# A hybrid decoder layer on one core: 32 groups by seven products instead of 25, with part of their sums on POOL

## The chip, the cores and the metric

The kernel runs on one core of a Trainium2 chip. The engines of the core that matter here are PE (TensorE: matmuls, and its weight loads, PEld), DVE (VectorE: elementwise work), ACT (ScalarE: elementwise work and copies), POOL (GpSimd: elementwise work) and SP (SyncE, which here only issues DMAs). SBUF is the memory on the core that all of them read and write; PSUM is the memory into which PE accumulates. The metric is the device time of one execution in microseconds; smaller is better.

## The reference

One decoder layer over 256 tokens and 2048 features, in float32. After an RMS norm one projection gives the inputs of a state-space mixer and of an attention mixer. Their outputs, 2048 features each, stand beside each other, and a matrix of 4096 x 2048 projects them out. A second RMS norm, a residual, and then an MLP:

```
mix = hybrid_mixer(rmsnorm(h, norm_mix_pre[i]), ...)      # ends in einsum('bse,ed->bsd', y_mix, w_out)
h = h + rmsnorm(mix, norm_mix_post[i])
hdn = relu(einsum('bsd,df->bsf', u, w_up))
ff = einsum('bsf,fd->bsd', hdn * hdn, w_down)             # w_down: 8192 x 2048
h = h + rmsnorm(ff, norm_mlp_post[i])
```

The change touches only the multiplications by w_out and w_down: activations of 256 tokens times weights, summed over 4096 and 8192 features.

## The kernel before, in words

**Two parts for each number.** A float32 matmul is done on operands split in two: `hi` is the value rounded to PE's faster format (ACT, line 136), `lo` is the rest (DVE, line 137, a subtraction of two operands in SBUF). A product is three matmuls: hi by hi, hi by lo, lo by hi. A matmul takes a 128x128 block of activations and a 128x512 block of weights.

**A plain group.** The sum over features goes in groups of 256 (two blocks of 128, KB = 2), and the output columns in blocks of 512. `row_tiles` does one group for one column block: a 512 KB tile of weights (`raw`) is loaded, split into a `hi` and a `lo` tile, and multiplied with both token blocks: 2 token blocks x 2 feature blocks x 3 matmuls = 12. `unit` treats two column blocks at once, so a plain group there has 24 matmuls and two raw tiles.

**A group by seven products.** For two token blocks, two feature blocks and two column blocks a group is a 2x2 by 2x2 block multiplication, eight products. `seven` (line 278) does it by Winograd's scheme with seven, 21 matmuls. For that it needs sums of blocks. Of the weights: with the raw tiles a and b, `e[:,0]` = a0 + b0, `e[:,1]` = e0 + b1, `t4` = e1 + a1, and b0 + b1 in place: four 128x512 additions on DVE (line 194), then splits of a, e, b (128x1024 each) and t4 (128x512), four hi/lo pairs. Of the activations: `sums_of_acts` (line 257 on) joins hi and lo (L269), takes three sums (L270 to L272) and splits the four results (L136, L137). These sums are kept in `room["sums"]` and used again when the second pair of column blocks comes. The seven products go partly into extra accumulators (`more`); a combination behind the last seven of a unit (`combine_new`, `combine_onto`) adds them up.

**The units.** There are six calls of `unit` with such groups: w_out, first and second pair of column blocks (lines 877 and 888); w_down's first 4096 rows (957, 959); its last 4096 rows (979, 983). Each has its order of groups with the list of those done by seven, and some last plain groups. Before these come five plain groups of w_out, beside which the attention ends.

**What sets the order.** The first part of every loop is the scheduler's: it places each instruction by priority and by its own estimate. The work on weights has a raised priority (AHEAD). For the groups in question `in_line` also puts each split and each addition of weights behind the last one on ACT and on DVE (`line`), so their order is that of the program. Loads go through SP's queue in program order. There are five pairs of hi and lo (BUFS), so a pair can be written only when PE is done with the pair five before. Of raw tiles there are four (RAWS), and, while the tile `u` of the layer's input isn't needed (w_out and the last part of w_down), three more in its memory. The memory of `u` holds the sums too: ten blocks (SUMS), two for each group. In the first part of w_down the memory of `h` holds eight (SUMS_H), and there are four raw tiles. The scratch tile `e` has one buffer, `r` (`tmp`) two; `wpost`, two tiles of 128x512, holds a norm's weights.

Of the kernel before, what the change touches and what calls it, by code (L numbers as in the profile page):

```python
# [10 lines left out]
F32 = mybir.dt.float32  # L11
F32R = mybir.dt.float32r
# [4 lines left out]
P = 128  # L17
# [31 lines left out]
WARM = 6  # L49
STAY = 4  # L50
SUMS = 10
SUMS_H = 8
FINE = 4


# [19 lines left out]
def hymba_layer(ctx: ExitStack, tc: tile.TileContext, x, norm_mix_pre, w_in, conv_w, conv_b, dt_bias, a_log,  # L75
# [17 lines left out]
    us = []  # L93

    def new_u():
        us[:] = [big.tile([P, n, 2, S], F32R, name=name) for n, name in ((SUMS, "ua"), (NK - SUMS, "ub"))]

    def u(k):

        return us[k // SUMS][:, k % SUMS]  # L100

    new_u()
    sh = big.tile([P, NK, S], F32R, name="sh")
# [43 lines left out]
        return raw  # L147


    room = {}  # L150

    def in_place_of_u():
        room["sums"] = big.tile([P, SUMS, 2, S], F32R, name="ua")
        room["raw"] = big.tile([P, NK - SUMS, NB], F32, name="ub")
        room["turn"] = 0
        sums_of.clear()

    def in_place_of_h():
        room["sums"] = hp.tile([P, SUMS_H, 2, S], F32R, name="h")
        room["raw"] = None  # L160
        sums_of.clear()

    def fetch_next(src, k0, c0):

        if room["raw"] is None:
            return fetch(src, k0, c0)
        n = KB * (room["turn"] - RAWS)
        room["turn"] = (room["turn"] + 1) % (RAWS + (NK - SUMS) // KB)
        return fetch(src, k0, c0, into=None if n < 0 else room["raw"][:, n:n + KB])

    def parts():
# [87 lines left out]
    def sums_of_acts(k):  # L259

        if k in sums_of:
            return sums_of[k]
        q = KB * len(sums_of)
        assert q < room["sums"].shape[1]
        h_, l_, r = part(k * KB)
        with tc.high_priority(offset=AHEAD):
            a, c = (tmp().rearrange("p (i s) -> p i s", s=P) for _ in range(2))
            ah_, al_ = (v[:, r:r + KB].bitcast(F32).rearrange("p j (t s) -> p (j t) s", t=NT) for v in (h_, l_))
            nc.vector.tensor_tensor(a, ah_, al_, op=ALU.add)  # L269
            nc.vector.tensor_tensor(c[:, 0:2], a[:, 0::3], a[:, 1:2].to_broadcast([P, 2, P]), op=ALU.subtract)  # L270
            nc.vector.tensor_tensor(c[:, 2], a[:, 0], c[:, 1], op=ALU.add)
            nc.vector.tensor_tensor(c[:, 3], a[:, 2], c[:, 2], op=ALU.subtract)  # L272
            ch, cl = (room["sums"][:, q + j].rearrange("p b (t s) -> p (b t) s", t=NT) for j in range(KB))
            split(ch, cl, c)
        sums_of[k] = ch, cl
        return ch, cl

    def seven(src, ca, cb, k, acc, more, first, last):
# [4 lines left out]
        with tc.high_priority(offset=AHEAD):  # L283
            raw_a = fetch_next(src, k * KB, ca)
            raw_b = fetch_next(src, k * KB, cb)
            e, t4 = hp.tile([P, KB, NB], F32, name="e"), tmp()
            add_in_line(e[:, 0], raw_a[:, 0], raw_b[:, 0])
            add_in_line(e[:, 1], e[:, 0], raw_b[:, 1])
            hl_a = parts()
            split_in_line(*hl_a, raw_a)  # L290
            add_in_line(t4, e[:, 1], raw_a[:, 1])
            add_in_line(raw_b[:, 0], raw_b[:, 0], raw_b[:, 1])
            hl_e = parts()
            split_in_line(*hl_e, e)
            hl_b = parts()
            split_in_line(*hl_b, raw_b)
            hl_t = parts()
            split_in_line(*(v[:, 0] for v in hl_t), t4)
# [66 lines left out]
                nc.vector.tensor_tensor(dst[:, f], a[:, 0], dst[:, f], op=ALU.add)  # L365

    def act_u(k):
        t = us[k // SUMS]
        return t[:, :, 0], t[:, :, 1], k % SUMS


    sq1 = cp.tile([P, NT, 4], F32, name="sq1")
# [501 lines left out]
    def order_of(ks, by_seven):  # L874
        return [(k, k in by_seven) for k in ks]

    unit(w_out, 0, order_of(range(early, 14), (6, 9, 12)), (14, 15), acc, more,
         lambda x: combine_new(0, x), 0, (whole(0), whole(1)), first=False)
    for n in (2, 3):
        load_wpost(norm_mix_post, n)  # L880
# [2 lines left out]
    def third(t, a):  # L883
# [1 line left out]
        first3.append(sums_but_last(ssq, t))  # L885

    first3 = []
    unit(w_out, 2, order_of((0, 1, 6, 2, 9, 3, 12, 5, 4, 7, 8, 10), (6, 9, 12, 4, 8)), (11, 13, 14, 15), acc, more,
         lambda x: combine_new(2, x), LAG_OUT, (third, done), 2)


# [47 lines left out]
    for hf in range(2):  # L939
# [14 lines left out]
        if hf == 0:  # L954
            in_place_of_h()
            acc, more = [bank() for _ in range(2 * NT)], [psmall(), bank(), psmall(), bank()]
            unit(w_down, 0, order_of(range(14), (4, 7, 10, 13)), (14, 15), acc, more,
                 lambda x: combine_new(0, x), 0, (onto(0), onto(1)))
            unit(w_down, 2, order_of((0, 1, 4, 2, 3, 7, 5, 6, 10, 8, 9, 13), (4, 7, 10, 13)), (11, 12, 14, 15), more, acc,
                 lambda x: combine_new(2, x), 0, (onto(2), onto(3)))  # L960
            h = hp.tile([P, NT, D], F32, name="h")

# [45 lines left out]
```

## Time and profile before

| what | before |
|---|---|
| median of 3 runs (lowest to highest) | 1496.34 us (1496.32 to 1499.82) |
| the profiled execution | 1494.86 us |
| its span, first to last instruction | 1493.1 us |
| mean granted clock of TensorE | 0.996 |
| matmuls | 7650 |
| busy: PE, DVE, ACT, POOL | 99%, 72%, 54%, 4% |
| the six units: w_out, w_down's first part, its last part | from 642 to 782, 968 to 1136, 1315 to 1483 us |

A row of the timeline has the start in us from the span's beginning, the duration in us, the engine, the line of the kernel, the operation, output<-inputs by their names in the program, and the shape; in brackets stands the idle time in front of it and what ended it. Matmuls overlap in the pipeline, so their spacing is the difference between starts. A row of a group has after the bar the busy time in us and the mean duration in ns, and then the idle time before.

### The profile page before, as it was taken

How to read it: one execution, taken by the hardware profiler on the slowest of the kernel's cores; microseconds unless marked ns; L12 is line 12 of the kernel's file. 1: busy time of each engine (PE TensorE's matmuls, PEld its weight loads, DVE VectorE, ACT ScalarE, POOL GpSimd, SP SyncE). 2: the span in 40 equal slices, each digit the busy share in tenths (PEclk: the TensorE clock that was granted, in tenths of full speed). 3: DMA queues.
4: the chain of work that ended last, by engine and by line, in shares of the span. 5: the costliest groups of instructions: out<-in, count | busy, mean ns of one | idle time of the engine just before them, and what ended most of it. 6: DMA issues, size and time to landing. Idle time of an engine off the chain costs nothing.

```text
span 1493.1 us, 20429 instructions
## 1 busy us (share of the span) xinstructions
PE 1477.8 (99%) x7650; PEld 1262.5 (85%) x7650; DVE 1075.3 (72%) x1582; ACT 806.0 (54%) x1125; POOL 56.9 (4%) x73
## 2 busy tenths in 40 slices
PE   9999999999999999999999999999999999999997
PEld 8888888888888888888878888888888888888886
DVE  6988897886555555587978656578775665678896
ACT  7574565455545454555556555545554554555552
POOL 0002200220000000000000000000000000000101
PEclk9999999999999999999999999999999999999999
DMA  7665666555656565575556666545568666656562
GB/s 275 196 201 181 182 185 189 179 169 169 178 167 178 170 171 180 204 247 199 199 188 208 194 189 190 185 169 197 200 213 273 189 184 194 187 203 206 198 214 97
DMA packets 151012, 287.35 MB, mean 192 GB/s; under 512 B 11664, under 2 KB 14592, under 8 KB 150656
## 3 DMA queue, kind: packets, MB, share of 16 engines
q1 hardware_dynamic: 143312, 272.37, 57.9%
q10 hardware_dynamic: 7600, 13.68, 2.7%
q8 instruction: 60, 0.98, 0.3%
q14 instruction: 40, 0.33, 0.1%
HBM read 281.78 MB, written 4.23 MB: 192 GB/s over the span
## 4 chain that ended last, share of the span: by engine, by line
PE 94%; DVE 2%; DMA 1%; ACT 1%; issue 1%; SPq 0%; POOL 0%; POOLq 0%; DVEq 0%; ACTq 0%
PE acc L341 29%; PE acc L344 15%; PE acc L242 11%; PE acc L243 11%; PE acc L241 10%; PE ps L242 2%; PE ps L241 2%; PE ps L243 2%; PE acc L312 2%; PE acc L311 2%; PE acc L313 2%; DVE lo L137 1%; PE ps L662 1%; PE ps L312 1%; PE ps L313 1%; PE ps L311 1%
## 5 line engine op out<-in xcount | busy, mean ns | idle before, releaser
L137 DVE TENSOR_TENSOR lo<-raw,hi 128x1024 fp32r<-128x1024 f32 (+1 forms) x466 | 569.5, 1225 | 313.2 <-ACT hi L136 306.7
L136 ACT ACTIVATE hi<-raw 128x1024 fp32r<-128x1024 f32 (+1 forms) x466 | 490.1, 1055 | 463.5 <-PE acc L341 239.6
L341 PE MATMUL acc<-ua,hi 128*128 128x512 f32 x1240 | 333.7, 399 | 0.8 <-DVE ua L139 0.8
L341 PEld LDWEIGHTS acc<-ua,hi 128*128 128x128 f32 x1240 | 217.6, 189 | 34.7 <-DVE ua L139 1.0
L341 PE MATMUL acc<-ub,hi 128*128 128x512 f32 x744 | 205.5, 397 | 0.0
L344 PEld LDWEIGHTS acc<-ua,lo 128*128 128x128 f32 x1240 | 182.0, 189 | 21.1
L344 PE MATMUL acc<-ua,lo 128*128 128x256 f32 x1240 | 187.2, 281 | 0.0
L341 PEld LDWEIGHTS acc<-ub,hi 128*128 128x128 f32 x744 | 127.2, 189 | 16.3 <-issue 0.2
L344 PEld LDWEIGHTS acc<-ub,lo 128*128 128x128 f32 x744 | 114.3, 189 | 15.8
L344 PE MATMUL acc<-ub,lo 128*128 128x256 f32 x744 | 118.1, 281 | 0.0
L241 PE MATMUL acc<-hi,sh 128*128 128x512 f32 x224 | 88.3, 394 | 0.0
L242 PE MATMUL acc<-lo,sh 128*128 128x512 f32 x224 | 87.3, 390 | 0.1
L243 PE MATMUL acc<-hi,sl 128*128 128x512 f32 x224 | 87.3, 390 | 0.0
L242 PE MATMUL acc<-lo,ah 128*128 128x512 f32 x208 | 81.0, 390 | 0.0
L243 PE MATMUL acc<-hi,al 128*128 128x512 f32 x208 | 80.9, 389 | 0.0
L241 PE MATMUL acc<-hi,ah 128*128 128x512 f32 x208 | 80.9, 389 | 0.0
L241 PE MATMUL acc<-hi,ua 128*128 128x512 f32 x180 | 71.2, 396 | 0.0
L242 PE MATMUL acc<-lo,ua 128*128 128x512 f32 x180 | 70.6, 392 | 0.0
L243 PE MATMUL acc<-hi,ua 128*128 128x512 f32 x180 | 70.5, 393 | 0.0
L137 DVE TENSOR_TENSOR lo<-ub,hi 128x1024 fp32r<-128x1024 f32 x48 | 58.4, 1221 | 16.5 <-ACT hi L136 15.8
L136 ACT ACTIVATE hi<-ub 128x1024 fp32r<-128x1024 f32 x48 | 50.2, 1056 | 36.5 <-PE acc L243 17.1
L136 ACT ACTIVATE hi<-e 128x1024 fp32r<-128x1024 f32 x25 | 26.6, 1062 | 47.0 <-DVE e L194 41.2
(315 smaller groups left out, 2114.4 us busy)
## 6 DMA issues: line engine op xcount, KB each, us to landing
raw<-in_w_in_dram SPq DMA_DIRECT2D x190, 512.0 KB, 3.6
raw<-in_w_up_dram SPq DMA_DIRECT2D x128, 512.0 KB, 3.7
raw<-in_w_down_dram SPq DMA_DIRECT2D x104, 512.0 KB, 4.4
raw<-in_w_out_dram SPq DMA_DIRECT2D x40, 512.0 KB, 4.1
ub<-in_w_out_dram SPq DMA_DIRECT2D x24, 512.0 KB, 4.2
ub<-in_w_down_dram SPq DMA_DIRECT2D x24, 512.0 KB, 4.5
bc<-acs_d ACTq DMA_DIRECT2D x8, 512.0 KB, 4.6
xs<-in_x_dram SPq DMA_DIRECT2D x8, 256.0 KB, 6.4
```

The lines of the kernel that those rows point to most:

```text
L136: return (nc.scalar.activation(hi, src, AF.Copy), nc.vector.tensor_tensor(lo, src, hi.bitcast(F32), op=ALU.subtract))
L137: nc.vector.tensor_tensor(lo, src, hi.bitcast(F32), op=ALU.subtract))
L241: nc.tensor.matmul(acc[t], a_h[:, r, ts], hi[:, j], start=begin, stop=False)
L242: nc.tensor.matmul(acc[t], a_h[:, r, ts], lo[:, j], start=False, stop=False)
L243: nc.tensor.matmul(acc[t], a_l[:, r, ts], hi[:, j], start=False, stop=end)
L311: nc.tensor.matmul(dst, a_h, hi[:, j], start=own and first, stop=False)
L312: nc.tensor.matmul(dst, a_h, lo[:, j], start=False, stop=False)
L313: nc.tensor.matmul(dst, a_l, hi[:, j], start=False, stop=own and last)
L341: nc.tensor.matmul(acc[f], hi[:, j, f * P:(f + 1) * P], u(k0 + j), start=k0 + j == 0, stop=False, skip_group_check=True)
L344: nc.tensor.matmul(acc[f][:, 0], lo[:, j, f * P:(f + 1) * P], u(k0 + j)[:, 0], start=False, stop=k0 + j == NK - 1, skip_group_check=True)
L662: nc.tensor.matmul(p[:, c, r], bc[:, r, c * P:(c + 1) * P], xdt[:, c, r], start=True, stop=True)
```

## The change

It does four things.

- 32 groups by seven in place of 25: the six units have 4, 6, 5, 5, 6, 6 where they had 3, 5, 4, 4, 4, 5. Between two sevens there is now mostly one plain group, where there were two in most units.
- In `seven`, two of the four additions of weights (b0 + b1, and t4) are given to POOL, and stand in front of a's split in the program; they are no longer in the line of DVE's instructions.
- In `sums_of_acts` the three sums behind the first go to POOL; joining hi and lo, and the split, stay.
- More groups have sums to keep: twelve blocks in the memory of `u` (ten and two more), so two raw tiles remain there where there were three; in the first part of w_down eight blocks in the memory of `h`, and two in the tiles of `wpost`.

```
-SUMS_H = 8
...
     def in_place_of_u():
-        room["sums"] = big.tile([P, SUMS, 2, S], F32R, name="ua")
-        room["raw"] = big.tile([P, NK - SUMS, NB], F32, name="ub")
+        a, b = big.tile([P, SUMS, 2, S], F32R, name="ua"), big.tile([P, KB, 2, S], F32R, name="ub")
+        room["sums"] = [a[:, k] for k in range(SUMS)] + [b[:, k] for k in range(KB)]
+        room["raw"] = big.tile([P, NK - SUMS - KB, NB], F32, name="uc")
...
     def in_place_of_h():
-        room["sums"] = hp.tile([P, SUMS_H, 2, S], F32R, name="h")
+        a = hp.tile([P, NK // 2, 2, S], F32R, name="h")
+        room["sums"] = [a[:, k] for k in range(NK // 2)]
+        room["sums"] += [hp.tile([P, 2, S], F32R, name="wpost", bufs=2) for _ in range(2)]
...
-        room["turn"] = (room["turn"] + 1) % (RAWS + (NK - SUMS) // KB)
+        room["turn"] = (room["turn"] + 1) % (RAWS + (NK - SUMS) // KB - 1)
...
             nc.vector.tensor_tensor(a, ah_, al_, op=ALU.add)
-            nc.vector.tensor_tensor(c[:, 0:2], a[:, 0::3], a[:, 1:2].to_broadcast([P, 2, P]), op=ALU.subtract)
-            nc.vector.tensor_tensor(c[:, 2], a[:, 0], c[:, 1], op=ALU.add)
-            nc.vector.tensor_tensor(c[:, 3], a[:, 2], c[:, 2], op=ALU.subtract)
+            nc.gpsimd.tensor_tensor(c[:, 0:2], a[:, 0::3], a[:, 1:2].to_broadcast([P, 2, P]), op=ALU.subtract)
+            nc.gpsimd.tensor_tensor(c[:, 2], a[:, 0], c[:, 1], op=ALU.add)
+            nc.gpsimd.tensor_tensor(c[:, 3], a[:, 2], c[:, 2], op=ALU.subtract)
...
             add_in_line(e[:, 1], e[:, 0], raw_b[:, 1])
+            nc.gpsimd.tensor_tensor(raw_b[:, 0], raw_b[:, 0], raw_b[:, 1], op=ALU.add)
+            nc.gpsimd.tensor_tensor(t4, e[:, 1], raw_a[:, 1], op=ALU.add)
             hl_a = parts()
             split_in_line(*hl_a, raw_a)
-            add_in_line(t4, e[:, 1], raw_a[:, 1])
-            add_in_line(raw_b[:, 0], raw_b[:, 0], raw_b[:, 1])
...
-    unit(w_out, 0, order_of(range(early, 14), (6, 9, 12)), (14, 15), acc, more,
+    unit(w_out, 0, order_of(range(early, 14), (6, 8, 10, 12)), (14, 15), acc, more,
...
-    unit(w_out, 2, order_of((0, 1, 6, 2, 9, 3, 12, 5, 4, 7, 8, 10), (6, 9, 12, 4, 8)), (11, 13, 14, 15), acc, more,
+    unit(w_out, 2, order_of((0, 1, 6, 2, 8, 3, 10, 5, 12, 7, 4, 9), (6, 8, 10, 12, 4, 9)), (11, 13, 14, 15), acc, more,
...
-            unit(w_down, 0, order_of(range(14), (4, 7, 10, 13)), (14, 15), acc, more,
+            unit(w_down, 0, order_of(range(14), (4, 6, 8, 10, 12)), (14, 15), acc, more,
...
-            unit(w_down, 2, order_of((0, 1, 4, 2, 3, 7, 5, 6, 10, 8, 9, 13), (4, 7, 10, 13)), (11, 12, 14, 15), more, acc,
+            unit(w_down, 2, order_of((0, 1, 4, 2, 6, 3, 8, 5, 10, 7, 12, 9), (4, 6, 8, 10, 12)), (11, 13, 14, 15), more, acc,
...
-    unit(w_down[4096:], 0, order_of(range(13), (3, 6, 9, 12)), (13, 14, 15), acc, more,
+    unit(w_down[4096:], 0, order_of(range(14), (3, 5, 7, 9, 11, 13)), (14, 15), acc, more,
...
-    unit(w_down[4096:], 2, order_of((0, 3, 1, 6, 2, 9, 4, 12, 5, 7, 8, 10), (3, 6, 9, 12, 8)), (11, 13, 14, 15), more, acc,
+    unit(w_down[4096:], 2, order_of((0, 1, 3, 2, 5, 4, 7, 6, 9, 8, 11, 13), (3, 5, 7, 9, 11, 13)), (10, 12, 14, 15), more, acc,
```

More of the change, by code (lines that the diff above doesn't have):

```diff
@@ L95, in new_u @@
     def new_u():
-        us[:] = [big.tile([P, n, 2, S], F32R, name=name) for n, name in ((SUMS, "ua"), (NK - SUMS, "ub"))]
+        a, b, c = (big.tile([P, n, 2, S], F32R, name=name)
+                   for n, name in ((SUMS, "ua"), (KB, "ub"), (NK - SUMS - KB, "uc")))
+        us[:] = [(a, k) for k in range(SUMS)] + [(b, k) for k in range(KB)] + [(c, k) for k in range(NK - SUMS - KB)]
     def u(k):
-        return us[k // SUMS][:, k % SUMS]
+        t, i = us[k]
+        return t[:, i]
     new_u()
@@ L262, in sums_of_acts @@
             return sums_of[k]
-        q = KB * len(sums_of)
-        assert q < room["sums"].shape[1]
+        places = room["sums"][2 * len(sums_of):][:2]
         h_, l_, r = part(k * KB)
@@ L269, in sums_of_acts @@
             nc.vector.tensor_tensor(a, ah_, al_, op=ALU.add)
[L270 to L273, printed above, removed]
+            nc.gpsimd.tensor_tensor(c[:, 0:2], a[:, 0::3], a[:, 1:2].to_broadcast([P, 2, P]), op=ALU.subtract)
+            nc.gpsimd.tensor_tensor(c[:, 2], a[:, 0], c[:, 1], op=ALU.add)
+            nc.gpsimd.tensor_tensor(c[:, 3], a[:, 2], c[:, 2], op=ALU.subtract)
+            ch, cl = (v.rearrange("p b (t s) -> p (b t) s", t=NT) for v in places)
             split(ch, cl, c)
@@ L367, in act_u @@
     def act_u(k):
-        t = us[k // SUMS]
-        return t[:, :, 0], t[:, :, 1], k % SUMS
+        t, i = us[k]
+        return t[:, :, 0], t[:, :, 1], i
     sq1 = cp.tile([P, NT, 4], F32, name="sq1")
```

## The prediction

> **What bounds the kernel now.** I read the page's busy shares and its chain of work first, to name the engine; then the timeline of PE inside the stages that the change touches, to see whether PE ever waits there; then a table of stretches and the timeline of DVE, to see how far its feeder is from its limit.
>
> ```profile
> PE 1477.8 (99%) x7650; PEld 1262.5 (85%) x7650; DVE 1075.3 (72%) x1582; ACT 806.0 (54%) x1125; POOL 56.9 (4%) x73
> PE 94%; DVE 2%; DMA 1%; ACT 1%; issue 1%; SPq 0%; POOL 0%; POOLq 0%; DVEq 0%; ACTq 0%
> ```
>
> PE is busy 99% of the span and is 94% of the chain. So only fewer matmuls, or a new wait in front of PE, can move the time.
>
> ```profile
> 716.38 0.39 PE L311 MATMUL acc<-hi,ah 128*128 128x512 f32 x1
> ...
> 721.14 0.39 PE L241 MATMUL ps<-hi,sh 128*128 128x512 f32 x1
> ...
> 726.58 0.39 PE L311 MATMUL acc<-hi,ah 128*128 128x512 f32 x1
> ```
>
> These are starts of PE in the second half of the output projection. A group by seven products runs from 716.38 to 721.14: 21 matmuls in 4.76 us, 0.2267 us each (the 0.39 us shown is the length of one in the pipeline, not the spacing). The plain group behind it has 24 matmuls and takes 5.44 us to 726.58. Nothing is lost between them: one seven and one plain group make a cycle of 10.20 us.
>
> ```profile
> 642.94:751.74 108.80, 108.80 (x481) 1.00 0.61 205
> 726.58:736.78 10.20, 10.20 (x46) 8.45 (x45) 10.10 (x16) 6.36 (x7) 0.00 (x0) 1.00 0.59 199
> ```
>
> In the table of stretches (length, then PE's busy time; in the second row PE, PEld, DVE, ACT and POOL) PE is busy for all of 108.80 us that hold eight sevens, at a granted clock of 1.00. In the 10.20 us cycle DVE is busy 10.10 us. PE sets the pace and DVE is only a little quicker.
>
> **The change part by part.** *Seven more sevens* (32 for 25), each with three matmuls less: 7 x 3 x 0.2267 = 4.76 us off the path, 0.32%. This is the whole gain, and it holds only if DVE still delivers.
>
> *DVE's work in a cycle.* This is one cycle of DVE before, where the next seven's sums of activations are new:
>
> ```profile
> 720.23 0.69 DVE L194 TENSOR_TENSOR e<-raw 128x512 f32<-128x512 f32 x1
> 720.95 0.69 DVE L194 TENSOR_TENSOR e<-e,raw 128x512 f32<-128x512 f32 x1
> 721.56 1.22 DVE L137 TENSOR_TENSOR lo<-raw,hi 128x1024 fp32r<-128x1024 f32 x1
> 722.69 0.68 DVE L194 TENSOR_TENSOR r<-e,raw 128x512 f32<-128x512 f32 x1
> 723.30 0.68 DVE L194 TENSOR_TENSOR raw<-raw 128x512 f32<-128x512 f32 x1
> 723.90 1.22 DVE L137 TENSOR_TENSOR lo<-e,hi 128x1024 fp32r<-128x1024 f32 x1
> 725.03 0.69 DVE L269 TENSOR_TENSOR r<-sh,sl 128x512 f32<-128x512 f32 x1
> 725.63 1.22 DVE L137 TENSOR_TENSOR lo<-raw,hi 128x1024 fp32r<-128x1024 f32 x1
> 726.77 0.68 DVE L137 TENSOR_TENSOR lo<-r,hi 128x512 fp32r<-128x512 f32 x1
> 727.49 0.42 DVE L270 TENSOR_TENSOR r<-r 128x256 f32<-128x256 f32 x1
> 727.95 0.29 DVE L271 TENSOR_TENSOR r<-r 128x128 f32<-128x128 f32 x1
> 728.16 1.22 DVE L137 TENSOR_TENSOR lo<-raw,hi 128x1024 fp32r<-128x1024 f32 x1
> 729.29 0.28 DVE L272 TENSOR_TENSOR r<-r 128x128 f32<-128x128 f32 x1
> 729.49 1.22 DVE L137 TENSOR_TENSOR lo<-raw,hi 128x1024 fp32r<-128x1024 f32 x1
> 730.63 0.68 DVE L137 TENSOR_TENSOR ua<-r,ua 128x512 fp32r<-128x512 f32 x1
> 731.23 0.68 DVE L194 TENSOR_TENSOR e<-ub 128x512 f32<-128x512 f32 x1
> ```
>
> From one e to the next is 11.0 us, against PE's 10.20. DVE issues the next instruction before the last one's end, so I count by starts: 0.60 for a 128x512, 1.14 for a 128x1024. The change takes from DVE the two additions of weights at 722.69 and 723.30 (1.20 us) and the three of activations (L270 to L272: 0.46, 0.21 and 0.20, together 0.87 us), 2.07 us in all. They go to POOL. What do they cost there?
>
> ```profile
> L969 POOL TENSOR_TENSOR mw<-mw,wpost x6: 1282/1596/2038, 1397.3 to 1475.2; 128x512 f32<-128x512 f32 x6
> L658 POOL TENSOR_TENSOR xs<-xs,yo 128x256 f32<-128x256 f32 x8 | 5.8, 725 | 33.0 <-DVE yo L656 33.0
> L137 DVE TENSOR_TENSOR lo<-raw,hi 128x1024 fp32r<-128x1024 f32 (+1 forms) x466 | 569.5, 1225 | 313.2 <-ACT hi L136 306.7
> ```
>
> ```profile
> 113.03 2.12 DVE L647 TENSOR_TENSOR bc<-bc,cbm 128x512 f32<-128x512 f32 x2
> 113.55 2.08 POOL L638 TENSOR_TENSOR xs<-xs,skip_b 128x256 f32<-128x256 f32 x2
> 115.08 1.63 DVE L137 TENSOR_TENSOR lo<-raw,hi 128x1024 fp32r<-128x1024 f32 x1
> ...
> 1397.34 2.04 POOL L969 TENSOR_TENSOR mw<-mw,wpost 128x512 f32<-128x512 f32 x1 [592.81 <-ACT junk L968]
> 1398.15 1.77 DVE L194 TENSOR_TENSOR r<-e,raw 128x512 f32<-128x512 f32 x1
> 1399.84 0.68 DVE L194 TENSOR_TENSOR ub<-ub 128x512 f32<-128x512 f32 x1
> ...
> 1401.96 1.46 POOL L969 TENSOR_TENSOR mw<-mw,wpost 128x512 f32<-128x512 f32 x1 [2.59 <-ACT junk L968]
> 1402.18 1.28 DVE L966 TENSOR_TENSOR mw<-acc,mw 128x512 f32<-128x512 f32 x2
> ```
>
> This is what decides the case. POOL and DVE don't run beside each other when a DVE instruction reads two operands in SBUF. At 1398.15 an addition of weights, the very kind at issue, holds DVE 1.69 us until the next start, where the same instruction at 722.69 took 0.61: one POOL 128x512 costs DVE 1.08 us. At 115.08 a split took 1.63 instead of 1.225 behind a 128x256 on POOL, 0.41 us, and the two products at 113.03 took 1.025 each in place of 0.60, 0.42 us. At 1402.18 two additions that read one operand from PSUM ran beside POOL in 1.28 together, undisturbed. Nearly all of DVE's work in these stages has both operands in SBUF. So an addition moved to POOL doesn't leave DVE free for 0.60 us: it stops it for 1.08. The 128x128 isn't shown on POOL; its bounds are 0 and the 0.42 of a 128x256, and I take half of that, 0.21, by its size.
>
> The Trainium skill's page "SBUF — State Buffer", section "Who interferes with whom", has the rule: a DVE instruction with two SBUF inputs contends with a GpSimd instruction that reads SBUF, one with a single SBUF input doesn't. The trace agrees on both halves (1.63 against 1.225 us; 1.28 us for two undisturbed). Without the rule, that is with POOL beside DVE, the cycle would be 8.9 us and the change a clean gain.
>
> *The cycle after, with new sums:* 11.0 - 2.07 + 2 x 1.08 + 0.42 + 2 x 0.21 = 11.93 us, 1.73 over PE's 10.20. *Without new sums:* less 2 x 0.60 and 0.84, 9.89 us, which PE covers.
>
> *How much lead hides it.* PE's five hi/lo pairs let DVE run ahead only so far.
>
> ```profile
> 717.72 2.58 DVE L137 TENSOR_TENSOR lo<-ub,hi 128x1024 fp32r<-128x1024 f32 x2 [0.85 <-ACT hi L136]
> ```
>
> The plain group that PE starts at 721.14 has its first split done at 717.72 + 1.22 = 718.94, and PE needs it for its second matmul at 721.37: a lead of 2.4 us, which can't be larger because ACT waited for the pair until PE had freed it. Over n cycles with new sums PE stalls n x 1.73 - 2.4. Before, two such cycles at most followed each other (2 x 0.8), so nothing showed. Now, by unit:
>
> - output projection, first half (sevens at 6, 8, 10, 12, a plain group between): the sums of the first are made during earlier plain groups, three cycles remain: 2.8 us.
> - second half: the sums stand already up to 12; then 7 plain, 4 and 9 by seven with new sums and nothing between. DVE and POOL need 2.28 + 2 x (9.89 - 2.28) + 2 x 2.04 = 21.6 us, PE 5.44 + 2 x 4.76 = 14.96: 6.6 less the lead, 4.2 us.
> - down projection, first 4096 rows, first half (4 to 12): four cycles, 4.5 us.
> - its second half: no new sums, but four raw tiles, all used in one cycle. The next seven's e can't start before b's split has freed its tile and a load has landed:
>
> ```profile
> raw<-in_w_down_dram SPq DMA_DIRECT2D x24, 512.0 KB, 4.7
> ```
>
>   From e to b's last split is 726.85 - 720.23 - 0.60 (the sum between) = 6.02 us before, 6.02 - 1.20 + 2.16 = 6.98 after, and 4.7 for the load: 11.7 us in place of 10.2, four times, less 2.4: 3.6 us. Its lower bound is 0, if loads land sooner.
> - last 4096 rows, first half (3 to 13): five cycles, 6.3 us. Second half: sums stand, 0.
>
> Together 21.4 us. *Other parts, at nothing:* ACT, which has the same conversions per group as before, is busy 6.36 of 10.20 us; POOL's own queue holds 4.0 us of work a cycle at the rows' lone durations, in the order b's sum, the last sum of weights, three sums of activations, and only the products of L969 stand among them; one raw tile less leaves six where a cycle uses four; three new places for sums are only addresses; the longer combination behind the last seven (with two plain groups in place of three after it) needs eight DVE instructions of 0.60, 4.8 us, against 2 x (5.44 - 2.28) = 6.3 us of slack, thin cover; if it's gone, up to 4.8 us.
>
> **The sum:** profiled execution 1494.86 us (span 1493.1 and 1.8 around it; 1.5 under the median of the runs, 1496.34) - 4.76 + 21.4 = 1511.5 us.
>
> **The rivals.** *POOL's work is hidden* (the other side): PE never waits, 1494.86 - 4.76 = 1490.1. For it: DVE's count falls to 8.9 us a cycle. It decides if a POOL 128x512 takes under 0.2 us from DVE (11.93 - 2 x 0.86 is PE's 10.20); the row at 1398.15 shows 1.08. Chance 0.13.
>
> *About even.* The stop costs only about what DVE is spared, 0.60 for a 128x512: cycle 10.97, 0.77 over. Then the units stall 0, 2.3, 0.7, 0 and 1.5 us, together 4.5: 1494.6. POOL may find gaps in which DVE waits for ACT, but in the cycle above there is hardly one. Chance 0.11.
>
> *POOL's whole duration counts*, not the 1.08 seen: 1.28 alone for a 128x512 (the least of L969), 0.72 for a 128x256 (L658), half for a 128x128. The cycle is 8.93 + 2.56 + 0.72 + 0.72 = 12.93, 2.73 over: stalls of 5.8, 6.2, 8.5, 5.2 and 11.3 us, 37 in all, and 1527. A chain from POOL through ACT that leaves DVE waiting would come to the same. Against it: the two rows that let the price be seen show less. The page named above says that the loser waits for the whole instruction; that is this rival. Chance 0.14.
>
> **How the numbers follow.** The forecast, DVE stopped by POOL as the rows price it, has 0.62; its own range is 1502 (a lead of 3.9 instead of 2.4 in each unit and no stall for the loads) to 1516 (the combination's 4.8 us uncovered). Hidden 0.13, even 0.11, whole duration 0.14. The range, 1490 to 1525, leaves out most of the last rival and little else. A change within 0.3% (4.5 us) can't be told from none here; the hidden case is just beyond it: faster 0.14, same 0.11, slower 0.75.
>
> **What would show it.** Right: POOL's busy time rises by 106 us (64 additions of 1.28, 17 sums of 1.44) or more; L194 and L137 on DVE show means above 0.69 and 1.22 us in these stages; PE, unbroken before, has idle time ended by DVE's lo in the first halves, growing along a unit, and least in the last second half. Sevens still take 4.76 us where fed. Wrong: DVE's means unchanged beside a busy POOL; or stalls ended by DMA or by POOL itself instead.

## The result and the profile after

The changed kernel takes 1534.65 us (median; 1533.42 to 1535.75) where the kernel before, run beside it, takes 1496.80: a ratio of 1.0254, with an interval of 1.0241 to 1.0266. The direction was forecast, the size was not: 37.9 us slower, not 15, and beyond the range's end of 1525. The profiled execution took 1533.42 us, its span is 1531.6, against 1494.86 and 1493.1 before. TensorE's mean granted clock is 0.997, where it was 0.996.

From the page of the changed kernel, the busy time of each engine and its chain of work by engine:

```profile
PE 1486.7 (97%) x7629; PEld 1255.3 (82%) x7629; DVE 1121.9 (73%) x1524; ACT 819.8 (54%) x1142; POOL 222.2 (15%) x188
DVE 4%; PE 2%; POOL 2%; issue 2%; ACT 1%; DMA 0%; POOLq 0%; ACTq 0%; DVEq 0%
```

The 21 matmuls are gone (7629 for 7650). The chain's shares can't be set beside the 94% that PE had before: those listed add up to 11% of the span and cover its last stretch only, which runs through DVE, POOL and ACT as well. POOL is busy 165 us more. The list of what PE waited for names one feeder above all (columns: us in total, times, longest; its two longest rows):

```profile
PE acc L317 <- DVE lo L139: 15.3, 18, 1.6
PE acc L248 <- DVE lo L139: 6.7, 9, 0.8
```

(In the changed kernel the splits stand at L138 and L139, DVE's additions of weights at L200, those on POOL at L294 and L295, the sums of activations at L274 to L277, the matmuls of a seven at L316 to L318 and those of a plain group at L247 to L249.)

The list counts only time in which PE is empty; the overlap of matmuls (0.39 us long, 0.2267 apart) hides the first 0.16 us of each stall. So I also summed, from the starts of PE, what lies over 0.2267 us per matmul in each unit:

| PE's stalls, us | forecast | changed kernel |
|---|---|---|
| output projection, first half | 2.8 | 6.1 |
| output projection, second half | 4.2 | 6.3 |
| down projection, first part, first half | 4.5 | 9.9 |
| down projection, first part, second half | 3.6 | 1.6 |
| down projection, last part, first half | 6.3 | 16.3 |
| down projection, last part, second half | 0 | 4.1 |
| together (before rounding) | 21.4 | 44.2 |

Before, these units held 0.9. 44.2 - 0.9 - 4.76 of matmuls saved is 38.5 us, which is the difference of the spans, 1531.6 - 1493.1. The whole loss lies in these units, and 18.7 of the 22.8 us that the forecast lacks lie in the three first halves.

Two cycles in the table of stretches (length, then busy time with count of PE, PEld, DVE, ACT and POOL, the granted clock, DMA share, GB/s), the first with new sums of activations, the second without:

```profile
1390.03:1403.87 13.84, 11.33 (x46) 8.21 (x45) 11.17 (x11) 6.23 (x8) 6.62 (x6) 1.00 0.46 152
1093.05:1103.24 10.19, 10.19 (x46) 8.45 (x45) 9.07 (x8) 5.91 (x6) 3.98 (x2) 1.00 0.60 199
```

Without new sums PE keeps its 10.20 us, as forecast. With them the cycle takes 13.84 where 11.93 was forecast. And DVE, the feeder, isn't full: 11.17 of 13.84. Its timeline in that cycle shows why:

```profile
1388.61 2.32 DVE L139 TENSOR_TENSOR lo<-raw,hi 128x1024 fp32r<-128x1024 f32 x1
1390.86 1.77 DVE L274 TENSOR_TENSOR r<-ah,al 128x512 f32<-128x512 f32 x1
1392.55 1.22 DVE L139 TENSOR_TENSOR lo<-e,hi 128x1024 fp32r<-128x1024 f32 x1
...
1394.82 0.68 DVE L139 TENSOR_TENSOR lo<-r,hi 128x512 fp32r<-128x512 f32 x1
1395.42 1.21 DVE L139 TENSOR_TENSOR lo<-raw,hi 128x1024 fp32r<-128x1024 f32 x1
1399.02 0.69 DVE L139 TENSOR_TENSOR ua<-r,ua 128x512 fp32r<-128x512 f32 x1 [2.38 <-ACT ua L138]
1399.97 1.23 DVE L139 TENSOR_TENSOR lo<-raw,hi 128x1024 fp32r<-128x1024 f32 x1 [0.26 <-ACT hi L138]
```

The first two rows are the stops that were forecast: 2.32 us where the kernel before has 1.22, and 1.77 where it has 0.68, 1.10 and 1.09 us for a 128x512 on POOL (1.08 forecast). The last two were not: DVE stands 2.38 + 0.26 us in front of the split of the sums (`ua<-r,ua`), with the splits that PE waits for queued behind it. POOL and ACT in the same stretch:

```profile
1388.05 1.80 POOL L294 TENSOR_TENSOR raw<-raw 128x512 f32<-128x512 f32 x1 [3.56 <-DVE e L200]
1389.81 2.27 POOL L295 TENSOR_TENSOR r<-e,raw 128x512 f32<-128x512 f32 x1
1395.58 1.65 POOL L275 TENSOR_TENSOR r<-r 128x256 f32<-128x256 f32 x1 [3.51 <-DVE lo L139]
1397.32 0.46 POOL L276 TENSOR_TENSOR r<-r 128x128 f32<-128x128 f32 x1
1397.86 0.47 POOL L277 TENSOR_TENSOR r<-r 128x128 f32<-128x128 f32 x1
```

```profile
1398.35 0.63 ACT L138 ACTIVATE ua<-r 128x512 fp32r<-128x512 f32 x1 [4.67 <-POOL r L277]
```

POOL's three sums start only at 1395.58, released by the split of `t4` (`lo<-r,hi`): of the scratch tile `r` there are two, and the sums need the one that `t4` holds. Then they take 2.8 us on POOL and 0.6 on ACT, and DVE's queue, which is in order, has only one split to do meanwhile. In all, the list of what DVE waited for has 29.4 us in front of the sixteen splits of sums (`ua` 14.2, `h` 8.9, `ub` 3.9, `wpost` 2.4), where the kernel before has 4.2 us in front of its thirteen, never more than 0.7 at once. The sum comes out: 11.93 forecast, less 0.84 (the stops that the three sums were to cause fall into DVE's idle time), plus 2.64, is 13.73; measured 13.84.

### The profile page after: what moved, and what is told of

Read it like the earlier page. It is cut to its first block, busy times and chain, and to the rows that moved or that the text cites. A ratio compares the mean times of both kernels' runs of the same rounds, so it can differ in the third digit from the quotient of the medians.

```text
span 1531.6 us, 20566 instructions
## 1 busy us (share of the span) xinstructions
PE 1486.7 (97%) x7629; PEld 1255.3 (82%) x7629; DVE 1121.9 (73%) x1524; ACT 819.8 (54%) x1142; POOL 222.2 (15%) x188
## 5 line engine op out<-in xcount | busy, mean ns | idle before, releaser
L139 DVE TENSOR_TENSOR lo<-raw,hi 128x1024 fp32r<-128x1024 f32 (+1 forms) x478 | 606.9, 1272 | 302.2 <-ACT hi L138 299.8
L138 ACT ACTIVATE hi<-raw 128x1024 fp32r<-128x1024 f32 (+1 forms) x478 | 502.5, 1055 | 437.5 <-PE acc L346 243.0
L346 PE MATMUL acc<-uc,hi 128*128 128x512 f32 x496 | 140.8, 396 | 0.0
L275 POOL TENSOR_TENSOR r<-r 128x256 f32<-128x256 f32 x17 | 21.7, 1275 | 725.7 <-DVE al L139 383.6
L349 PEld LDWEIGHTS acc<-uc,lo 128*128 128x128 f32 x496 | 80.3, 189 | 13.4
L346 PEld LDWEIGHTS acc<-uc,hi 128*128 128x128 f32 x496 | 82.5, 189 | 8.1
L247 PE MATMUL acc<-hi,sh 128*128 128x512 f32 x212 | 83.8, 395 | 0.3 <-ACT hi L138 0.3
L349 PE MATMUL acc<-uc,lo 128*128 128x256 f32 x496 | 83.4, 280 | 0.0
L249 PE MATMUL acc<-hi,sl 128*128 128x512 f32 x212 | 82.7, 390 | 0.0
L247 PE MATMUL acc<-hi,ua 128*128 128x512 f32 x180 | 71.3, 396 | 0.0
L249 PE MATMUL acc<-hi,ua 128*128 128x512 f32 x180 | 70.3, 392 | 0.0
L247 PE MATMUL acc<-hi,ah 128*128 128x512 f32 x176 | 69.1, 393 | 0.0
L249 PE MATMUL acc<-hi,al 128*128 128x512 f32 x176 | 68.5, 389 | 0.0
L138 ACT ACTIVATE hi<-e 128x1024 fp32r<-128x1024 f32 x32 | 34.0, 1062 | 59.4 <-DVE e L200 57.6
L346 PE MATMUL acc<-ub,hi 128*128 128x512 f32 x248 | 64.7, 399 | 0.0
```

The source lines that it names most:

```text
L138: return (nc.scalar.activation(hi, src, AF.Copy), nc.vector.tensor_tensor(lo, src, hi.bitcast(F32), op=ALU.subtract))
L139: nc.vector.tensor_tensor(lo, src, hi.bitcast(F32), op=ALU.subtract))
L247: nc.tensor.matmul(acc[t], a_h[:, r, ts], hi[:, j], start=begin, stop=False)
L249: nc.tensor.matmul(acc[t], a_l[:, r, ts], hi[:, j], start=False, stop=end)
L275: nc.gpsimd.tensor_tensor(c[:, 0:2], a[:, 0::3], a[:, 1:2].to_broadcast([P, 2, P]), op=ALU.subtract)
L346: nc.tensor.matmul(acc[f], hi[:, j, f * P:(f + 1) * P], u(k0 + j), start=k0 + j == 0, stop=False, skip_group_check=True)
```

## The experiments

Ratios are to the kernel before, run beside each; brackets are 95% intervals. The first three kernels undo parts of the change.

**The sums of activations back on DVE.**

```
-            nc.gpsimd.tensor_tensor(c[:, 0:2], a[:, 0::3], ...)      # and the two behind it
+            nc.vector.tensor_tensor(c[:, 0:2], a[:, 0::3], ...)
```

> The changed kernel with the three sums of activations back on DVE; the two additions of weights stay on POOL. Theory A (the chain): in the changed kernel a cycle of one seven and one plain group with new sums takes 13.8 us, of which DVE spends 2.4 + 0.26 us idle at the split of the sums, because the first sum on POOL waits until the last weight sum has left one of the two scratch tiles r, and the sums then go through three POOL instructions and ACT. With the sums on DVE they need no POOL; DVE's work is 11.0 - 1.20 + 2 x 1.09 = 12.0 us, with at most the 0.96 us of idle time that the kernel before has at the same split: stalls of 22 to 33 us, time 1512 to 1524. Theory B (the stop alone: POOL's holds on DVE, in whatever places, make all of the loss): the holds of 2 x 1.09 remain and the sums' 0.87 return to DVE, so the cycle stays at 13.8 or rises: 1530 to 1540.

1518.63 us, 1.0148 [1.0131, 1.0165]: in the range of theory A. DVE's timeline of a cycle:

```profile
1388.00 0.69 DVE L200 TENSOR_TENSOR e<-uc 128x512 f32<-128x512 f32 x1
...
1389.33 2.32 DVE L139 TENSOR_TENSOR lo<-uc,hi 128x1024 fp32r<-128x1024 f32 x1
1391.57 1.77 DVE L274 TENSOR_TENSOR r<-ah,al 128x512 f32<-128x512 f32 x1
...
1398.38 0.68 DVE L139 TENSOR_TENSOR ub<-r,ub 128x512 fp32r<-128x512 f32 x1
1400.12 0.68 DVE L200 TENSOR_TENSOR e<-raw 128x512 f32<-128x512 f32 x1
```

The two stops stay, the wait is gone, and from e to e it takes 12.12 us instead of 13.83. The additions of weights alone on POOL cost by their stops.

**The additions of weights back on DVE**, in their old place.

```
-            nc.gpsimd.tensor_tensor(raw_b[:, 0], raw_b[:, 0], raw_b[:, 1], op=ALU.add)
-            nc.gpsimd.tensor_tensor(t4, e[:, 1], raw_a[:, 1], op=ALU.add)
             hl_a = parts()
             split_in_line(*hl_a, raw_a)
+            add_in_line(t4, e[:, 1], raw_a[:, 1])
+            add_in_line(raw_b[:, 0], raw_b[:, 0], raw_b[:, 1])
```

> The changed kernel with the two additions of weights back on DVE, in its line; the three sums of activations stay on POOL. Theory A (the chain through the scratch tile and POOL): the idle time of 2.6 us at the split of the sums stays, the holds of 2 x 1.09 become 2 x 0.60: cycle 12.8, 2.6 over PE's in the first halves, and no stall in the last second half: 30 us of stalls, about 1520 (1515 to 1526). Theory B (the stop by the additions of weights is all of it): the cycle falls to 11.0 - 0.87 + 0.84, 11.0 us, stalls of 5 us: 1495 to 1500.

1515.34 us, 1.0130 [1.0115, 1.0146]: theory A again. Here it is the other way round: the stops are gone (the same split of a takes 1.22), the wait stays. DVE, then POOL:

```profile
1389.58 1.22 DVE L139 TENSOR_TENSOR lo<-uc,hi 128x1024 fp32r<-128x1024 f32 x1
...
1400.13 0.69 DVE L139 TENSOR_TENSOR ub<-r,ub 128x512 fp32r<-128x512 f32 x1 [2.38 <-ACT ub L138]
```

```profile
1395.62 2.73 POOL L275 TENSOR_TENSOR r<-r 128x256 f32<-128x256 f32 x1 [8.68 <-DVE lo L139]
```

POOL was idle for 8.68 us before it could begin, and the first sum then takes 2.73 us beside two splits of 128x1024 on DVE. So the wait isn't POOL's load; it comes from when the sums may start and from what stands behind their split.

**Nothing on POOL**: both edits together, so that only 32 sevens, their orders and the memory remain of the change.

> The changed kernel with nothing on POOL: 32 sevens, the new orders and the new memory, all sums on DVE as in the kernel before. By the count of DVE's starts a cycle with new sums is 11.0 us, 0.8 over PE's, and one without 8.9: stalls of 5 us at least, 1495, and with the 0.96 us of idle time that the kernel before shows at the split of the sums 15 us, 1505. If it is at or below the kernel before (1492 to 1497), the sevens and their places are sound and POOL alone makes the loss; if it is above 1515, the orders themselves are what costs and POOL's part is small.

1499.57 us, 1.0020 [1.0011, 1.0029]. With the two above this makes a square: weights on POOL add 19.1 us (1518.63 - 1499.57), sums on POOL 15.8, both 35.1 (1534.65 - 1499.57), which is the sum of the two. The moves to POOL cost 35 of the 38 us. The sevens themselves don't gain yet either: PE's stalls in the units are 7.4 us, more than the 4.76 saved. Two places hold most of them, and they come back further down. (That the square closes so exactly is in part chance: in the profiled executions TensorE's clock stood at half inside the units for 6.8 us with only the weights on POOL and for 3.4 us with nothing there, and not at all in the other two kernels.)

**A scratch tile of its own for `t4`**, to let the sums start earlier.

```
-            e, t4 = hp.tile([P, KB, NB], F32, name="e"), tmp()
+            e, t4 = hp.tile([P, KB, NB], F32, name="e"), cst[:, P:P + NB]
```

> The changed kernel with one edit: the last sum of weights (t4) has a place of its own, in a part of the constants' tile that nothing reads behind attention, so that the sums of activations no longer wait for its split. Everything stays on POOL. Theory A: the sums run ahead, DVE's idle time at their split goes, and the cycle comes to what the rows price, 11.9 us: stalls of 16 to 24 us, 1506 to 1514. Theory B: POOL holds DVE as long as before, 13.8 us a cycle, within 0.3% of the changed kernel, 1530 to 1538.

1525.21 us, 1.0193 [1.0178, 1.0208]: neither theory; 9.4 us less than the changed kernel, a quarter of its loss. With the scratch free, the scheduler places the sums of several groups in a lump, and in such a lump DVE stands in front of each of their splits as before:

```profile
996.06 0.69 DVE L139 TENSOR_TENSOR h<-r,h 128x512 fp32r<-128x512 f32 x1 [2.37 <-ACT h L138]
...
1005.07 0.69 DVE L139 TENSOR_TENSOR wpost<-r,wpost 128x512 fp32r<-128x512 f32 x1 [2.34 <-ACT wpost L138]
```

Over all sixteen splits DVE's idle time falls to 15.2 us, about half of the 29.4, but 8.2 us now stand at the joins (L274), which wait for POOL's last sum; there it was 1.9. So my theory that the two scratch tiles alone cause the wait falls. They set when the chain starts; that DVE waits for it comes, by these rows, from the place of the split, at the head of DVE's queue right behind the start of the chain. The next kernel tests that. (In the profiled execution the clock also stood at half for 17 us inside the units, where the changed kernel's stayed at 1.00: 12 us of this with PE at work, some 6 us lost. Without that loss the time would still be above the theory's 1514.)

**The split of the sums later.** This is the changed kernel with one edit: POOL's sums are issued as before, but their split goes in line behind the split of a in the seven that needs them.

```
             ch, cl = (v.rearrange("p b (t s) -> p (b t) s", t=NT) for v in places)
-            split(ch, cl, c)
+        to_split[k] = ch, cl, c
...
             split_in_line(*hl_a, raw_a)
+            if k in to_split:
+                split_in_line(*to_split.pop(k))
```

> The changed kernel; only the split of the activations' sums stands later on ACT and DVE: in their line, right behind a's split of the seven that needs it, not where the scheduler puts it. All sums stay on POOL. Theory A (DVE stands at that split, at the head of its queue, while three POOL instructions and ACT are still to come): the idle time of 2.4 + 0.26 us in a cycle goes, and the holds stay: cycle 13.8 - 2.6 + at most 0.84 for holds that fell into idle time before, 11.2 to 12.0, stalls of 16 to 24 us, 1506 to 1515. Rival B (the idle time only moves to another wait on POOL, such as the last sum of weights): above 1525.

1519.85 us, 1.0158 [1.0144, 1.0172]: 14.8 us less than the changed kernel, with the same instructions. The cycle is as expected, the total 5 us over the range. In front of the sixteen splits of sums DVE has no idle time left. DVE in the cycle that stood idle 2.6 us above:

```profile
1386.77 0.94 DVE L200 TENSOR_TENSOR e<-uc 128x512 f32<-128x512 f32 x1
1387.75 0.84 DVE L200 TENSOR_TENSOR e<-e,uc 128x512 f32<-128x512 f32 x1
1388.51 2.32 DVE L139 TENSOR_TENSOR lo<-uc,hi 128x1024 fp32r<-128x1024 f32 x1
1390.75 1.77 DVE L139 TENSOR_TENSOR ua<-r,ua 128x512 fp32r<-128x512 f32 x1
1392.44 1.21 DVE L139 TENSOR_TENSOR lo<-e,hi 128x1024 fp32r<-128x1024 f32 x1
...
1395.92 2.90 DVE L139 TENSOR_TENSOR lo<-raw,hi 128x1024 fp32r<-128x1024 f32 x2
1398.74 0.95 DVE L200 TENSOR_TENSOR e<-raw 128x512 f32<-128x512 f32 x1
```

No row has idle time in front. From e to e it takes 11.97 us; the prediction's sum gave 11.93. The stops that the wait had swallowed are back (0.94 and 0.84 for 0.69, 2.90 for two splits that take 2.36 undisturbed). PE's stalls in the three first halves are now 2.2, 4.0 and 7.0 us, where the prediction had 2.8, 4.5 and 6.3 and the changed kernel has 6.1, 9.9 and 16.3.

What is left over the forecast lies in the last second half, 4.0 us for 0 (as in the changed kernel, which comes further down), and in the output projection's second half, 8.7 us for 4.2, where the changed kernel has 6.3. POOL's timeline there, and DVE's:

```profile
751.23 1.32 POOL L277 TENSOR_TENSOR r<-r 128x128 f32<-128x128 f32 x1
752.63 0.46 POOL L278 TENSOR_TENSOR r<-r 128x128 f32<-128x128 f32 x1
753.17 1.27 POOL L296 TENSOR_TENSOR r<-e,raw 128x512 f32<-128x512 f32 x1
```

```profile
755.14 0.69 DVE L139 TENSOR_TENSOR lo<-r,hi 128x512 fp32r<-128x512 f32 x1 [2.90 <-ACT hi L138]
```

In this kernel `t4` (L296) stands behind the three sums of the next seven in POOL's queue, and its split at the head of DVE's: the same fault one engine further on. PE was nearly empty for several us, and then the granted clock fell, as the table of stretches shows:

```profile
757.00:760.00 3.00, 0.58 (x1) 0.50 (x2) 3.00 (x3) 2.10 (x2) 3.00 (x2) 0.73 0.67 244
760.00:762.00 2.00, 2.00 (x6) 1.32 (x4) 2.00 (x2) 1.47 (x2) 0.50 (x1) 0.50 0.00 0
762.00:766.00 4.00, 4.00 (x11) 3.03 (x11) 4.00 (x5) 2.60 (x4) 0.00 (x0) 0.60 0.00 2
```

**POOL's part alone**: the kernel before, with its 25 sevens, orders and memory, and only the additions and sums moved to POOL.

> The kernel before, with its 25 sevens, its orders and its memory, and only the moves to POOL: two additions of weights, three sums of activations. The cycle of one seven and two plain groups is 15.64 us on PE; with the holds and the idle time of the changed kernel's cycle (13.8 us with one plain group) DVE would need 13.8 + 2.28 = 16.1, 0.4 over, which the lead covers for four cycles; the stretch of the output projection with two new sums and one plain group between needs 2 x 3.6 - 2.4, 5 us. Theory: the moves alone cost 4 to 9 us, 1500 to 1505, far less than the 35 that they cost with 32 sevens, since there DVE has slack. Rival (the moves cost the same each time): 25/32 of 35 us, 27: 1523.

1516.40 us, 1.0137 [1.0124, 1.0151], over the theory's 1505 and below the rival's 1523. I had counted on the two plain groups between sevens to cover the wait; they don't. In the first part of the down projection:

```profile
1018.39 0.69 DVE L137 TENSOR_TENSOR h<-r,h 128x512 fp32r<-128x512 f32 x1 [2.59 <-ACT h L136]
1019.33 4.63 DVE L137 TENSOR_TENSOR lo<-raw,hi 128x1024 fp32r<-128x1024 f32 x4 [0.25 <-ACT hi L136]
1026.95 0.69 DVE L194 TENSOR_TENSOR e<-raw 128x512 f32<-128x512 f32 x1 [2.99 <-DMA raw<-in_w_down_dram]
```

From e to e it takes 19.37 us (the e before stands at 1007.58), against PE's 15.64. DVE stands 2.59 + 0.25 us at the split of the sums, the four splits behind it come later by as much, and DVE then stands 2.99 us more for the next seven's load. A wait for that load is there without POOL too (the kernel before has 18.2 us of it, in eight places). So the slack that I had counted on is a wait for loads; the rows suggest that it doesn't shrink when the splits come late, since a load can start only when a split has freed its raw tile. To see whether the place of the split is the cause here too, the same kernel with the split later:

```
-            split(ch, cl, c)
+        to_split[k] = ch, cl, c
...
             split_in_line(*hl_a, raw_a)
+            if k in to_split:
+                split_in_line(*to_split.pop(k))
```

> The kernel before with the moves to POOL (1516.4) and the split of the activations' sums set later in line, behind a's split of the seven that needs it. What is open: why the moves cost 20 us there although PE's cycle of 15.64 us leaves DVE slack. Theory (the wait at the head of DVE's queue holds up the splits of the plain groups behind it, so raw tiles come free late, and the next seven waits for its loads): without that wait DVE and POOL need 11.95 + 2.28 = 14.2 of 15.64 us, and only the stretch with two new sums in the output projection and the start of the last two column blocks still stall, 2 to 5 us: 1498 to 1502. Rival (the holds by POOL's weights' additions are what delays the loads): 1510 or more.

1500.41 us, 1.0025 [1.0015, 1.0034], as expected: 3.9 us over the kernel before, where it was 20.1. PE's stalls in the units fall from 23.8 to 4.2.

```profile
1017.64 0.69 DVE L194 TENSOR_TENSOR e<-raw 128x512 f32<-128x512 f32 x1 [2.36 <-DMA raw<-in_w_down_dram]
...
1018.98 2.32 DVE L137 TENSOR_TENSOR lo<-raw,hi 128x1024 fp32r<-128x1024 f32 x1
1021.22 1.77 DVE L137 TENSOR_TENSOR h<-r,h 128x512 fp32r<-128x512 f32 x1
```

The stops are there (2.32, 1.77), the sums' split has no idle time in front, and DVE's wait for the load, 2.36 us, is now slack: PE is busy throughout (15.60 of the 15.60 us from 1007.9 to 1023.5). So with 25 sevens the stops cost at most 3.9 us; nearly all the rest was the wait.

**Can the 32 sevens gain?** With nothing on POOL, two stalls were left: the two neighbouring sevens at the end of the output projection, and ACT standing at loads of the norm's weights (`load_wpost`, issued by ACT) that need POOL's products done. So: one plain group put between those sevens, and the loads called at the combination instead of before the unit.

```
-    unit(w_out, 2, order_of((0, 1, 6, 2, 8, 3, 10, 5, 12, 7, 4, 9), ...), (11, 13, 14, 15), ...
+    unit(w_out, 2, order_of((0, 1, 6, 2, 8, 3, 10, 5, 12, 7, 4, 11, 9), ...), (13, 14, 15), ...
...
-    for n in (2, 3):
-        load_wpost(norm_mlp_post, n)
...
-         lambda x: combine_onto(2, x), LAG_DOWN, (complete(2), finish))
+         lambda x: (load_wpost(norm_mlp_post, 2), load_wpost(norm_mlp_post, 3), combine_onto(2, x)), LAG_DOWN, ...
```

> The version with everything on DVE and 32 sevens (1499.6), with two edits: the loads of the last norm's weights for the last two column blocks are issued behind the last seven of that unit and not ahead of it, where ACT's queue waited for POOL's products; and a plain group stands between the two last sevens of the output projection. The first should take 4.4 us of stalls away, the second 1.6: 1493.5 (1492 to 1495.5), 0.2% under the kernel before. If the wait on ACT's queue was not the cause, 1498 or more.

1496.61 us, 1.0001 [0.9992, 1.0010]: not the gain that I expected. The first edit worked: that half's stalls went from 1.6 us to 0. The second did nothing, since the scheduler put the loads where they had been (the last second half has the same stalls as before, 2.8 us of them; its 4.4 had 3.4 us at half clock behind them). From ACT's timeline (the first row is its queue's issue of the load):

```profile
1409.43 0.33 ACTq L869 DMA_DIRECT2D wpost<-in_norm_mlp_post_dram  x1
1409.81 0.63 ACT L138 ACTIVATE hi<-r 128x512 fp32r<-128x512 f32 x1 [1.88 <-POOL mw L974]
```

Then with the loads tied behind the last split given to ACT:

```
+    def late_wpost():
+        with tc.issue_after(line["act"].ins):
+            for n in (2, 3):
+                load_wpost(norm_mlp_post, n)
...
+         lambda x: (late_wpost(), combine_onto(2, x)), LAG_DOWN, (complete(2), finish))
```

> As the version with the late load (all on DVE, 32 sevens, 1496.6), but the two loads of the norm's weights are tied behind the last split that ACT has been given at that point. In the version before the scheduler had still placed them at the old spot, and ACT's queue stood there for POOL's products: 2.8 us of stalls in front of the plain group behind the first seven. If ACT's queue is the cause, these 2.8 us go and the time is 1493 to 1495, 0.1 to 0.2% under the kernel before; if not, it stays at 1496 to 1498.

1492.69 us, 0.9973 [0.9963, 0.9983]: faster than the kernel before by 3.9 us and than the changed one by 42. The loads are now issued at 1460.2 and 1462.8, behind the unit's conversions, and the conversion of `t4` that stood there no longer waits:

```profile
1413.18 0.62 ACT L138 ACTIVATE hi<-r 128x512 fp32r<-128x512 f32 x1
```

PE's stalls in the units fell from 4.0 to 1.9 us, so of the 4.76 saved 3.8 should remain (4.76 - 1.9 + 0.9), which the medians show. That the loads gave 3.9 us by the medians and 2.1 by the stalls isn't traced. (The two profiled executions can't be compared in time: this one, at 1496.37 the longest of its nine, comes to the output projection 4.65 us later than the other, ahead of everything that the edit touches.)

**Sums on POOL with the split later, in that kernel** (the one before the tied loads): the place on POOL that should cost least.

```
-            nc.vector.tensor_tensor(c[:, 0:2], a[:, 0::3], ...)      # and the two behind it
+            nc.gpsimd.tensor_tensor(c[:, 0:2], a[:, 0::3], ...)
...
-            split(ch, cl, c)
+        to_split[k] = ch, cl, c        # split in line behind a's split, as above
```

> The same as the version with the late load and the spaced order, but the three sums of activations are on POOL and their split stands in line behind a's split of the seven that needs it. Theory A: without the wait at the head of DVE's queue the POOL sums cost DVE no more than the 0.87 us that they spare it, a cycle of 10.6 to 11.0 us: within 2 us of the version with all on DVE, 1491 to 1496. Rival: if POOL's sums cost DVE much by their holds, 1500 or more.

1497.93 us, 1.0011 [1.0002, 1.0020]: 1.3 us over the same kernel with the sums on DVE, within the 2 us expected, though above the 1491 to 1496. The sums cost 15.8 us on POOL with the split in its early place and about nothing with the late one, and they gain nothing either: the wait is still there in part (six times, 6.1 us in all, where the early place has 32).

```profile
1384.90 0.69 DVE L139 TENSOR_TENSOR ub<-r,ub 128x512 fp32r<-128x512 f32 x1 [1.02 <-ACT ub L138]
```

## Why the prediction was right in direction and wrong in size

**The gain** was right: 21 matmuls, 4.76 us, and the balance of stalls and gain meets the span to 0.1 us.

**The price of the stop** was right: 1.08 us from one row of the kernel before, 1.09 and 1.10 measured, in this kernel and in each with weights on POOL. The Trainium skill's page "SBUF — State Buffer", section "Who interferes with whom", by which a DVE instruction with two SBUF inputs contends with a POOL instruction that reads SBUF, fits: a's split took 2.32 us beside POOL's addition and 1.22 without it. That POOL loses time as well is more than I had used. The additions on POOL in the changed kernel (columns: count, busy us, mean ns, idle time before):

```profile
L295 POOL TENSOR_TENSOR r<-e,raw 128x512 f32<-128x512 f32 x23 | 50.9, 2214 | 2.0 <-issue 1.3 <-POOL raw L294 0.7
L294 POOL TENSOR_TENSOR raw<-raw 128x512 f32<-128x512 f32 x23 | 40.5, 1759 | 126.5 <-DVE e L200 114.5 <-DMA raw<-in_w_out_dram 6.2 <-DMA uc<-in_w_down_dram 5.8
```

They last 1.76 and 2.21 us, not 1.28, which is most of why POOL's busy time grew by 165 us instead of the 106 that I gave as the least.

**The step that failed is "The cycle after, with new sums".** It added up what DVE does and what POOL takes from it: 11.93 us. That is right for the work, as the kernel with the split later shows (11.97), and so is the lead of 2.4 us (first halves of 2.2, 4.0 and 7.0 against 2.8, 4.5 and 6.3). But it left out the wait that the move adds. Before, the three sums and their split stood on DVE in order, with only ACT's conversion between them, and DVE waited there for 0.7 us at most. Afterwards the split waits for POOL and ACT, at the head of DVE's queue, mostly for 2.4 us and once more 0.26 behind it, and the plain group's splits stand behind it. I had asked of each POOL operation what it takes from DVE, and not what is queued behind the instruction that waits for it. The first halves stalled 18.7 us more than the sum by this; with the wait taken away they stall 13.2 us together, where the sum had 13.6, and the total fell by 14.8. The signs that the prediction named for being right came all the same, but for the last second half, which wasn't the least: POOL's time rose, DVE's rows grew longer, PE waited for DVE's lo. They can't tell a stop of DVE from a wait of DVE; idle time in front of DVE's own rows does.

**"Other parts, at nothing"** held two more costs, 4.1 us in the last second half, forecast at 0. "POOL's own queue" was dismissed because only the products of the norm stand in it; they do, but ACT's queue stands at the loads that wait for those products, and PE needs what is behind them. POOL, ACT and DVE of the changed kernel:

```profile
1442.30 4.88 POOL L974 TENSOR_TENSOR mw<-mw,wpost 128x512 f32<-128x512 f32 x3
1448.09 1.79 POOL L974 TENSOR_TENSOR mw<-mw,wpost 128x512 f32<-128x512 f32 x1 [0.91 <-ACT junk L973]
```

```profile
1449.91 0.33 ACTq L869 DMA_DIRECT2D wpost<-in_norm_mlp_post_dram  x1
1450.30 0.63 ACT L138 ACTIVATE hi<-r 128x512 fp32r<-128x512 f32 x1 [2.28 <-PE acc L318]
```

```profile
1451.03 0.69 DVE L139 TENSOR_TENSOR lo<-r,hi 128x512 fp32r<-128x512 f32 x1 [2.29 <-ACT hi L138]
```

The split of `t4` waits for the conversion on ACT, which stands behind the load, which waits for the product that ended at 1449.88. (The row on ACT names PE, but it starts right behind the load's issue, which ended at 1450.24.) That costs 2.5 us, and the kernel with nothing on POOL has the same stall, so the moves to POOL aren't its cause; the two neighbouring sevens at that unit's end cost another 1.6, which my sum for it didn't contain.

**The sizes of two terms:** the output projection's second half was 6.3 for 4.2, and the four raw tiles of the first part's second half 1.6 for 3.6. The cycles there came near to the sum (from e to e 11.2 to 11.6 us behind the e at 1086.64, for 11.7), so more than 2.4 us of lead must have covered them; by how much isn't traced.

**The rivals.** "Hidden" and "about even" fell. "POOL's whole duration" came nearest in time (1527), by a price that is wrong (1.28 for 1.09). Its side remark, a chain from POOL through ACT that leaves DVE waiting, named the true mechanism, but I priced it by that rival's sum and gave it no chance of its own. Worked out like the rest, with the 2.64 us that only the changed kernel shows, it gives a cycle of 13.73, 3.53 over PE's; the twelve such cycles of the three first halves then stall 12 x 3.53 - 3 x 2.4 = 35.2 us in place of 13.6, and the forecast would have been 1533.

**What stays open:** how the stall of the output projection's second half divides between the stops and the wait; why the costs of the two moves add up so exactly, although in the changed kernel part of one falls into the idle time of the other (the clock has a part in it); and whether an order of sevens and loads made for POOL would cost less than these.

## What to carry to other kernels

An operation with two SBUF operands that is moved from DVE to POOL doesn't relieve DVE where DVE's own work has two SBUF operands: here it took 1.09 us from DVE to spare it 0.60. And when part of a chain moves to another engine, look at the instruction that consumes the result: in an in-order queue it makes everything behind it wait, so issue it late, just ahead of its own consumer; that alone gave back 14.8 us here with the same instructions. The same goes for a load on a compute engine's queue that waits for another engine's reader.

## What the runs showed of the hardware

**The granted clock halves behind stalls of PE.** In the kernel with the split later PE stood empty 4.2 us out of six (1.34, 0.23 and 2.58 us in front of three matmuls between 753.4 and 759.4), and then the granted clock is 0.73, 0.50 and 0.60 in the stretches shown above, while matmuls started every 0.43 us instead of 0.2267. The deficits (3 x 0.27 + 2 x 0.50 + 4 x 0.40) come to 3.4 us, so the clock stood at half for 6.8 us, from 758.4 to 765.2. PE was still empty for the first 1.0 us of these, so it is about 2.9 of that half's 8.7 us. Less was enough elsewhere: with nothing on POOL, stalls of 1.49 and 0.76 us in front of the matmuls at 1417.75 and 1419.01 are followed by a clock of 0.57 from 1419 to 1423, which is 3.4 us at half. In the units of the changed kernel no single stall is over 1.75 us, and the clock is 1.00 in all of them. How much idle time it takes, these runs don't settle. The Trainium skill's page "TensorE: Matmul & The Clock Gate", section "What's actually happening", has this: after an idle window of about 3.4 us the array gets half its clock until a busy window has passed. The trace agrees on the half and on the 3.4 us, once or twice that long, but not on a window that is idle throughout: in the 3.4 us ahead of 758.4 PE was busy for 1.46 us.

**POOL's small operations are stretched too.** A 128x256 sum that takes 0.72 us alone took 1.65 beside one split of DVE and 2.73 beside two.
